# The experts' gate and up weights, eight neighbouring rows to a partition, and modulated rows stored in the matching order

## The chip, the cores and the metric

The kernel runs on one core of one Trainium2 chip: TensorE (PE in the rows, its weight loads PEld), VectorE (DVE), ScalarE (ACT), GpSimd (POOL), SyncE (SP, which here only issues DMAs), and 16 DMA engines between the device memory and the core's on-chip memory of 128 partitions. The metric is the device time of one execution in microseconds. Before the change it is 4040.15 us, the median of three runs (4038.35 to 4043.37).

## The reference

Three layers work on 1024 tokens of 1024 features, all in float32. Each is a token mixer (neighbourhood attention in the first, grouped-query attention in the second, a mix of three kinds in the third), then a mixture of experts. What matters here is the part between the mixer and the experts, and the experts:

```
y = mixer(h)                                             # ends in @ w_o
x = layer_norm(alpha * x + (1 + g1) * y, ln_g, ln_b)
h = x * (1 + sc2) + sh2                                  # the modulated rows
y = hierarchical_moe(h, ...)

# hierarchical_moe: 32 experts in 4 groups; each token goes to its 2 best
xs = rows of h that the router sends to the expert
ys = (silu(xs @ w_gate[e]) * (xs @ w_up[e])) @ w_down[e]
out = sum over a token's two experts of gate * ys
```

`w_gate` and `w_up` of one expert are 1024x512 in the first two layers and 1024x256 in the third; `w_down` is 512x1024 and 256x1024. The products `xs @ w_gate[e]` and `xs @ w_up[e]` sum over the 1024 features, so any order of the features gives the same result as long as xs and the weights have the same one.

## The kernel before

Matrix products keep float32's precision by splitting each operand into a high and a low part: ACT copies the raw tile to the high part (H), DVE subtracts that from the raw tile for the low part (L), and PE adds three products (`mm3`, lines L181 to L183). In the expert stages ACT's copy is L2237 and DVE's subtraction L2246.

**Weights.** `Experts` holds for each layer a list of 1 MB pieces (`seq`): in the two wide layers (FF = 512) four pieces for gate and up and two for down an expert, in the narrow third layer (FF = 256) two pieces that hold gate and up side by side, and one for down. `load` issues the DMAs of the next piece on SP's queue (L2207, one function for all) into a ring of ten raw tiles R, as soon as an older piece has been split, so loads run some pieces ahead of their use. A piece of gate is 512 rows of the matrix: row k*128 + p of them goes to partition p, so a partition takes four separate rows of 512 floats (2 KB each) or, in the third layer, of 256 floats (1 KB each). `step` runs the matrix products of a piece; chunk q of the features, 128 of them, is on PE's rows.

**Tokens.** The modulated rows h2 lie in device memory. For each expert POOL gathers up to 128 of its tokens' rows (L2257, whole rows of 4 KB), and PE transposes them in eight chunks of 128 features (`turned`), the first chunk being features 0 to 127. If an expert has more than 128 tokens, `extra` runs an extra expert pass (`expert`) behind the stage; with these inputs there is one, in the third layer.

**The mixer's end.** `mixer_out` works through eight tiles of 128 tokens: output projection, layer norm, router. Its inner functions are generators that are advanced between the steps of the projection; the order on each engine is the order in which that code is written, and engines wait for each other by semaphores. Per tile: DVE adds the residual (L475, L478), the layer norm writes z, `modulated` writes h (L510: z times the row A on DVE; L512: plus the row B, on POOL, for the last two tiles on DVE) and stores it to h2 (L513); `last` makes the layer's x in z (L516, L518) and stores it (L519, `x<-z` in the rows). There are two z buffers, so L475 of a tile waits for the store of the tile two before. In the last tile of a routing group (t = 2, 5, 7) DVE runs the routing between these. The rows A and B, the same 1024 numbers in each partition, are made at the start of `mixer_out` by three DVE operations (L418 to L420). The router has weights and columns of its own and reads z, not h2. `ol` (L432) is the low part of the mixer's output, for which PE's first products wait.

Of the kernel before, what the change touches and what calls it, by code (L numbers as in the profile page):

```python
# [10 lines left out]
F32 = mybir.dt.float32  # L11
F32R = mybir.dt.float32r
# [4 lines left out]
ALU = mybir.AluOpType  # L17
# [5 lines left out]
P = 128  # L23
T = 1024
D = 1024
NT = T // P
NK = D // P
# [107 lines left out]
class K:  # L135
# [246 lines left out]
    def mixer_out(self, lay, x, ot, x1, h2, hi, pool, first, moe, done):  # L382
# [3 lines left out]
        nc, ps = self.nc, self.ps  # L386
        W, parts, live = {}, {}, []
# [23 lines left out]
        with self.tc.issue_after(ins.ins):  # L411
            G1, A, B = [self.row(q, lay.mod[j * D:(j + 1) * D], f"mod{j}") for q, j in ((first, 2), (pool, 4), (pool, 3))]
            g, b = self.row(pool, lay.ln1_g, "lng"), self.row(pool, lay.ln1_b, "lnb")
            rt = self.router_load(pool, lay, moe.hold)
        nc.vector.tensor_scalar_add(G1, G1, 1.0)

        t1 = pool.tile([P, D], F32, name="z", bufs=2)
        nc.vector.scalar_tensor_tensor(t1, A, 1.0, b, op0=ALU.add, op1=ALU.mult)  # L418
        nc.vector.tensor_add(B, B, t1)
        nc.vector.scalar_tensor_tensor(A, A, 1.0, g, op0=ALU.add, op1=ALU.mult)  # L420
        slots = ps.tile([P, 96], F32, name="R", bufs=1)
        finish, logits = [], []

# [12 lines left out]
        a, c = cols[:, 2], cols[:, 3]  # L436
# [17 lines left out]
        def rest(t, X, Y):  # L454
            s = slice(t * P, (t + 1) * P)
            end = t == NT - 1
            z = pool.tile([P, D], F32, name="z", bufs=2)
            st = pool.tile([P, 20], F32, name="lnst", bufs=4)
            hT = pool.tile([P, NK, P], F32, name="h2T", bufs=1)
            tp, lp = [None, None], []  # L460

            def logit(ks):
                if 0 in ks:
                    lp[:] = [ps.tile([P, 36], F32, name="O", bufs=1)]
                for k in ks:
                    nc.tensor.matmul(lp[0], hT[:, k, :], rw[:, 0, k], start=(k == 0), stop=(k == NK - 1))

            def turned(n):
                tp[n] = ps.tile([P, 4, P], F32, name="tp", bufs=2)
                for k in range(4 * n, 4 * n + 4):  # L470
                    nc.tensor.transpose(tp[n][:, k % 4, :], z[:, k * P:(k + 1) * P], self.ident)

            for n in range(2):
                f = slice(n * 512, (n + 1) * 512)
                nc.vector.tensor_mul(z[:, f], Y[n], G1[:, f])  # L475
                if n == 0:
                    yield
                nc.vector.scalar_tensor_tensor(z[:, f], X[:, f], lay.alpha, z[:, f], op0=ALU.mult, op1=ALU.add)  # L478
                yield
                if n and not end:  # L480
                    yield
                turned(n)
                nc.vector.bn_stats(st[:, 6 * n:6 * n + 6], z[:, f])
                if n == 0:
                    yield
                    nc.scalar.activation(hT[:, 0:4], tp[0], AF.Copy)
                    yield
                    if end:
                        logit(range(4))
            norm = self.normal(z, z, st)  # L490
            next(norm)
            yield
            nc.scalar.activation(hT[:, 4:8], tp[1], AF.Copy)
            next(norm)
            yield
            logit(range(4, 8) if end else range(8))
            next(norm)
            tb = pool.tile([P, 36], F32, name="rtb", bufs=2)
            nc.vector.scalar_tensor_tensor(tb, sums[:, 0], st[:, 17:18], sums[:, 1], op0=ALU.mult, op1=ALU.add)
            if t in starts:  # L500
                logits[:] = [pool.tile([P, 3, 36], F32, name="rL", bufs=2)]
            L = logits[0][:, t - groups[t][0]]
            yield
            run(norm)
            h = pool.tile([P, D], F32, name="h", bufs=1)

            late = t > NT - 3

            def modulated():
                nc.vector.tensor_mul(h, z, A)  # L510
                yield
                (nc.vector if late else nc.gpsimd).tensor_add(h, h, B)  # L512
                (nc.sync if end else nc.gpsimd).dma_start(h2[s], h)  # L513

            def last():
                nc.vector.tensor_mul(z, z, g)  # L516
                yield
                (nc.vector if late else nc.gpsimd).tensor_add(z, z, b)  # L518
                (nc.sync if late else nc.gpsimd).dma_start(x1[s], z)  # L519

            nc.vector.scalar_tensor_tensor(L, lp[0], st[:, 15:16], tb, op0=ALU.mult, op1=ALU.add)
            if t == groups[t][-1]:
                live.append(self.route(groups[t], logits[0], rt, self.tables[lay.l], pool, slots, modulated() if end else iter(())))
            yield
            if not end:
                run(modulated())
            yield
            if late:
                finish.append(last())
            else:  # L530
                run(last())
# [7 lines left out]
        with self.tc.manual_schedule(engines=MANUAL):  # L539
            for t in range(NT):  # L540
# [10 lines left out]
                for i in range(8):  # L551
                    n, j = i // 4, order[i % 4]
                    wh, wl = W[j]
# [541 lines left out]
    def apart(self, key, ins):  # L1095

        for o in self.groups.setdefault(key, []):
            self.tc.declare_no_dep(ins.ins, o.ins, reason="places of their own")
        self.groups[key].append(ins)
# [60 lines left out]
    def expert(self, x, gate, w_gate, w_up, w_down, g2, FF, raw, hi, wk):  # L1160
# [3 lines left out]
        if FF == 512:  # L1164
            for w in (w_gate, w_up):
                for j in range(2):
                    r = next(raw).tile([P, 4, 512], F32, name="R")
                    nc.sync.dma_start(r, w[j * 512:(j + 1) * 512].rearrange("(k p) f -> p k f", p=P))
                    gu.append(r)
        else:  # L1170
            for j in range(2):
                r = next(raw).tile([P, 4, 2, 256], F32, name="R")
                for a, w in enumerate((w_gate, w_up)):
                    nc.sync.dma_start(r[:, :, a], w[j * 512:(j + 1) * 512].rearrange("(k p) f -> p k f", p=P))
                gu.append(r.rearrange("p k a f -> p k (a f)"))
        for j in range(NF // 2):
            r = next(raw).tile([P, 2, D], F32, name="R")
            nc.sync.dma_start(r, w_down[j * 256:(j + 1) * 256].rearrange("(k p) f -> p k f", p=P))
# [8 lines left out]
            self.evac_split(tp, xh[:, 4 * g:4 * g + 4], xl[:, 4 * g:4 * g + 4])  # L1187
        acc = [ps.tile([P, 512], F32, name="pj", bufs=2) for _ in range(len(gu) // 2)]
        for j, r in enumerate(gu):
            wh, wl = self.split(r, *[hi.tile([P, 4, 512], F32R, name=n) for n in "HL"])  # L1190
            o = acc[j // 2]
            for c in range(4):
                k = 4 * (j % 2) + c
                self.mm3(o, xh[:, k], xl[:, k], wh[:, c], wl[:, c], k == 0, k == NK - 1)
        g, u = (acc[0], acc[1]) if FF == 512 else (acc[0][:, :256], acc[0][:, 256:])
        a = wk.tile([P, FF], F32, name="a", bufs=2)
        nc.scalar.activation(a, g, AF.Silu)
# [969 lines left out]
        es.close()  # L2167


class Experts:  # L2170


# [24 lines left out]
    def load(self, queue=None):  # L2197

        i = self.loaded
        place = RING[i % len(RING)]  # L2200
        if i == self.n or place == len(self.raw):
            return
        self.loaded += 1
        raw = self.raw[place]
        kind, e, j = self.seq[i]
        def start(out, in_):
            self.last = (queue or self.nc.sync).dma_start(out, in_)  # L2207

        gate, up, down = self.w
        if kind == "d":  # L2210
            r = raw.tile([P, 2, D], F32, name="R")
            start(r, down[e, j * 256:(j + 1) * 256].rearrange("(k p) f -> p k f", p=P))
        elif self.FF == 512:
            r = raw.tile([P, 4, 512], F32, name="R")
            start(r, (gate, up)[j // 2][e, j % 2 * 512:j % 2 * 512 + 512].rearrange("(k p) f -> p k f", p=P))
        else:
            r = raw.tile([P, 4, 2, 256], F32, name="R")
            for a in range(2):
                start(r[:, :, a], (gate, up)[a][e, j * 512:(j + 1) * 512].rearrange("(k p) f -> p k f", p=P))
            r = r.rearrange("p k a f -> p k (a f)")  # L2220
        self.R[i] = r

    def more(self, pool, px):
# [131 lines left out]
    def step(self, i):  # L2355
        kind, e, j = self.seq[i]
        k = self.k
        (self.wide if self.FF == 512 else self.narrow)(kind, e, j)
        if self.made < i + 4:
            self.make()  # L2360
        wh, wl = self.W.pop(i)
        if kind == "g":
            xh, xl = self.x[e]
            for c in range(4):
                q = 4 * (j % 2) + c
                k.mm3(self.acc[e][j // 2], xh[:, q], xl[:, q], wh[:, c], wl[:, c], q == 0, q == NK - 1)
        else:
            th, tl = self.th[e]
            for c in range(2):
                q = 2 * j + c  # L2370
                for n in range(2):
                    s = slice(n * 512, (n + 1) * 512)
                    k.mm3(self.out[e][n], th[:, q], tl[:, q], wh[:, c, s], wl[:, c, s], q == 0, q == self.NF - 1)
# [210 lines left out]
```

## Time and profile before

| | |
|---|---|
| median of 3 runs | 4040.15 us (4038.35 to 4043.37) |
| profiled execution | 4045.79 us, its span 4044.0 |
| PE busy | 3465.9 us (86%) |
| DVE busy | 3333.8 us (82%) |
| ACT busy | 2284.6 us (56%) |
| POOL busy | 1474.3 us (36%) |
| DMA | 880.07 MB, mean 218 GB/s; 551312 of 554644 packets under 8 KB, 280623 under 2 KB |
| mean granted TensorE clock | 0.925 of full speed |

The span runs from the first to the last instruction. Busy time is summed over an engine's instructions; the stages have different limits, so a share of the whole span does not tell what a stage waits for. In rows of the trace a name left of an arrow is what is written, the names to its right are what is read; a line L510 is a line of the kernel, sometimes of a helper. A number in brackets at the end of a row is how long the engine had been idle, and what ended that.

### The profile page before, as it was taken

Reading aid. Unit: us, or ns where it says so; the run is one execution under the profiler, and the core shown is the slowest. Engines: PE = TensorE matmul, PEld = TensorE weight load, DVE = VectorE, ACT = ScalarE, POOL = GpSimd, SP = SyncE. Lnnn points to the kernel's source line nnn. Section 1 sums busy time; section 2 is a strip of 40 time slices with the busy share of each in tenths; the row PEclk is TensorE's granted clock in tenths of the full one; section 3 lists DMA queues with packets and bytes.
Section 4 is the critical chain, followed back from the end, with each engine's and each line's share of the span. In section 5 each row is a group of like instructions: output and inputs, shape, how many; then the busy total and the mean of one; then the engine's idle time right before and its main releaser. Section 6 shows DMA issues by size and latency. Waiting matters only on the chain. (4 is left out here: it accounts for less than half of the span.)

```text
span 4044.0 us, 50699 instructions
## 1 busy us (share of the span) xinstructions
PE 3465.9 (86%) x17618; PEld 2823.9 (70%) x17618; DVE 3333.8 (82%) x4774; ACT 2284.6 (56%) x3295; POOL 1474.3 (36%) x1138
## 2 busy tenths in 40 slices
PE   5999877799999697999877999993989888869991
PEld 4777756688887576877666888872778666657771
DVE  6599967899998897999777999989445578679996
ACT  3377632577776456888425777764422366237762
POOL 2255413232222335867432322326122142233443
PEclk8999989899999798999998999996979999979996
DMA  8879673899998537434538999995100013559994
GB/s 265 237 142 165 153 184 108 303 379 373 373 376 314 201 123 242 139 115 128 173 107 298 377 369 372 377 335 181 47 14 1 27 50 110 176 163 342 335 350 178
DMA packets 554644, 880.07 MB, mean 218 GB/s; under 512 B 117167, under 2 KB 280623, under 8 KB 551312
## 3 DMA queue, kind: packets, MB, share of 16 engines
q1 hardware_dynamic: 477440, 747.48, 55.5%
q0 software_dynamic: 76944, 129.31, 10.7%
q8 instruction: 141, 2.31, 0.2%
q14 instruction: 119, 0.97, 0.1%
HBM read 791.89 MB, written 126.82 MB: 227 GB/s over the span
## 5 line engine op out<-in xcount | busy, mean ns | idle before, releaser
L2246 DVE TENSOR_TENSOR L<-R,H 128x2048 fp32r<-128x2048 f32 x480 | 1092.7, 2282 | 45.8 <-ACT H L2237 45.3
L2237 ACT ACTIVATE H<-R 128x2048 fp32r<-128x2048 f32 x480 | 918.7, 1916 | 198.5 <-PE R L183 80.6
L2300 POOL DMA_INDIRECT y<-O,slots x96 | 254.9, 2655 | 569.9 <-DVE O L2299 549.6
L2257 POOL DMA_INDIRECT X<-h,slots x87 | 182.0, 2092 | 465.6 <-PE tp L2269 438.8
L181 PE MATMUL pj<-H,xh 128*128 128x512 f32 x776 | 318.6, 411 | 7.9 <-ACT xh L195 5.4
L183 PE MATMUL pj<-H,xl 128*128 128x512 f32 x776 | 308.3, 397 | 19.3 <-DVE xl L196 19.3
L182 PE MATMUL pj<-L,xh 128*128 128x512 f32 x776 | 306.5, 395 | 1.8 <-DVE L L188 1.8
L195 ACT ACTIVATE ph<-tp 128x512 fp32r<-128x512 f32 (+1 forms) x352 | 199.5, 567 | 115.9 <-PE tp L1268 102.6
L359 POOL TENSOR_TENSOR macc<-macc,mw 128x512 f32<-128x512 f32 x182 | 237.1, 1303 | 71.0 <-ACT mw L355 61.6
L196 DVE TENSOR_TENSOR pl<-tp,ph 128x512 fp32r<-128x512 f32 (+1 forms) x352 | 224.7, 645 | 25.3 <-ACT ph L195 23.7
L1252 DVE TENSOR_REDUCE st<-S 128x1 f32<-128x1024 f32 (+2 forms) x192 | 204.1, 1063 | 21.5 <-PE S L1558 18.6
L181 PE MATMUL S<-H,xh 128*128 128x512 f32 x512 | 211.9, 414 | 0.0
L195 ACT ACTIVATE xh<-tp 128x512 fp32r<-128x512 f32 x194 | 115.4, 597 | 166.4 <-PE tp L2269 103.5
L183 PE MATMUL S<-H,xl 128*128 128x512 f32 x512 | 201.7, 394 | 0.0
L182 PE MATMUL S<-L,xh 128*128 128x512 f32 x512 | 199.6, 390 | 0.0
L183 PEld LDWEIGHTS pj<-H,xl 128*128 128x128 f32 x776 | 147.8, 190 | 53.9 <-DVE xl L196 20.7
L181 PEld LDWEIGHTS pj<-H,xh 128*128 128x128 f32 x776 | 148.3, 191 | 35.9 <-ACT xh L195 6.2
L1268 PE MATMUL tp<-ident,E 128*128 128x128 f32 x1111 | 171.7, 273 | 0.5 <-DVE pl L196 0.5
L1279 PE MATMUL O<-ph,V 128*128 128x512 f32 (+1 forms) x352 | 163.2, 464 | 10.4 <-DVE U L1286 10.4
L182 PEld LDWEIGHTS pj<-L,xh 128*128 128x128 f32 x776 | 148.6, 191 | 30.3 <-DVE L L188 2.1
L1268 PEld LDWEIGHTS tp<-ident,E 128*128 128x128 f32 x1111 | 139.2, 141 | 37.0 <-DVE pl L196 1.7
L1262 ACT ACTIVATE E<-S,st 128x1024 f32<-128x1024 f32 (+6 forms) x149 | 157.1, 1054 | 12.0 <-DVE st L1252 10.8
(592 smaller groups left out, 9877.7 us busy)
## 6 DMA issues: line engine op xcount, KB each, us to landing
R<-moe_w_down SPq DMA_DIRECT2D x161, 1024.0 KB
R<-moe_w_up SPq DMA_DIRECT2D x127, 1024.0 KB
R<-moe_w_gate SPq DMA_DIRECT2D x126, 1024.0 KB
mw<-ada_w SPq DMA_DIRECT2D x160, 256.0 KB
R<-moe_w_gate SPq DMA_DIRECT2D x66, 512.0 KB
R<-moe_w_up SPq DMA_DIRECT2D x66, 512.0 KB
Y<-y SPq DMA_DIRECT2D x24, 1024.0 KB
mw<-w_mod SPq DMA_DIRECT2D x96, 256.0 KB
```

The source lines that it names most:

```text
L181: mm(out, ah, bh, start=first, stop=False)
L182: mm(out, ah, bl, start=False, stop=False)
L183: mm(out, al, bh, start=False, stop=last)
L195: nc.scalar.activation(hi, src, AF.Copy)
L196: nc.vector.tensor_sub(lo, src, hi.bitcast(F32))
L359: nc.gpsimd.tensor_add(acc, acc, W)
L1252: nc.vector.tensor_reduce(blk.st[:, a, 0:1], S[:, :n], axis=AX.X, op=ALU.max, negate=True)
L1268: nc.tensor.transpose(tp[:, a, :], blk.E[a][:, c * P:(c + 1) * P], self.ident)
L2237: self.nc.scalar.activation(hi, r, AF.Copy)
L2246: self.nc.vector.tensor_sub(lo, r, hi.bitcast(F32))
L2257: return self.nc.gpsimd.indirect_dma_start(out=self.X[e % 3], out_offset=None, in_=self.h2d, in_offset=IOA(ap=i, axis=0), bounds_check=T - ...
L2300: ins = nc.gpsimd.indirect_dma_start(out=self.y, out_offset=IOA(ap=self.slots.bitcast(I32)[:, 1, e:e + 1], axis=0), in_=O, in_offset=None, ...
```

## The change

Row 8p + k of gate or up, instead of row k*128 + p, goes to partition p: a partition holds eight neighbouring rows, which come in two pieces of four. The four rows are one stretch in device memory, 8 KB in the wide layers and 4 KB in the third, where gate and up now lie one behind the other in the raw tile (2, 4, 256) instead of side by side (4, 2, 256), and PE's moving operand is two runs of 256 columns. Chunk k of the features is then 8p + k for p = 0 to 127. For the tokens' rows to match, `modulated` writes h in eight pieces of 128, piece k from every eighth number of z; A and B are brought into that order once a layer by two copies, and the sums that A and B come from are made in the tile z first. Down weights are as before. The same is done in the extra pass.

```diff
         t1 = pool.tile([P, D], F32, name="z", bufs=2)
+        apart = lambda v: v.rearrange("t (p k) -> t k p", k=NK)
+        pieces = lambda v: v.rearrange("t (k p) -> t k p", k=NK)
         nc.vector.scalar_tensor_tensor(t1, A, 1.0, b, op0=ALU.add, op1=ALU.mult)
-        nc.vector.tensor_add(B, B, t1)
-        nc.vector.scalar_tensor_tensor(A, A, 1.0, g, op0=ALU.add, op1=ALU.mult)
+        nc.vector.tensor_add(t1, t1, B)
+        nc.vector.tensor_copy(pieces(B), apart(t1))
+        t1 = pool.tile([P, D], F32, name="z", bufs=2)
+        nc.vector.scalar_tensor_tensor(t1, A, 1.0, g, op0=ALU.add, op1=ALU.mult)
+        nc.vector.tensor_copy(pieces(A), apart(t1))
...
             def modulated():
-                nc.vector.tensor_mul(h, z, A)
+                nc.vector.tensor_mul(pieces(h), apart(z), pieces(A))
...
+def rows_of(w, j):
+    return w.rearrange("(p k) f -> p k f", k=NK)[:, 4 * j:4 * j + 4]
...
         elif self.FF == 512:
             r = raw.tile([P, 4, 512], F32, name="R")
-            start(r, (gate, up)[j // 2][e, j % 2 * 512:j % 2 * 512 + 512].rearrange("(k p) f -> p k f", p=P))
+            start(r, rows_of((gate, up)[j // 2][e], j % 2))
         else:
-            r = raw.tile([P, 4, 2, 256], F32, name="R")
+            r = raw.tile([P, 2, 4, 256], F32, name="R")
             for a in range(2):
-                start(r[:, :, a], (gate, up)[a][e, j * 512:(j + 1) * 512].rearrange("(k p) f -> p k f", p=P))
-            r = r.rearrange("p k a f -> p k (a f)")
+                start(r[:, a], rows_of((gate, up)[a][e], j))
...
-                k.mm3(self.acc[e][j // 2], xh[:, q], xl[:, q], wh[:, c], wl[:, c], q == 0, q == NK - 1)
+                w = [v[:, c] if self.FF == 512 else v[:, :, c] for v in (wh, wl)]
+                k.mm3(self.acc[e][j // 2], xh[:, q], xl[:, q], *w, q == 0, q == NK - 1)
```

The order of instructions changes on DVE at the start of each `mixer_out` alone. The second layer's start on DVE, before; `mod_18608` is the row A, `mod_18610` the row B, `rab` and `rcols` belong to the router:

```order
L188 TENSOR_TENSOR L<-R,H 128x2048 x4
L418 SCALAR_TENSOR_TENSOR z<-mod_18608,lnb 128x1024
L438 SCALAR_TENSOR_TENSOR rab<-rcols 128x8
L432 TENSOR_TENSOR ol<-o,oh 128x512
L419 TENSOR_TENSOR mod_18610<-mod_18610,z 128x1024
L420 SCALAR_TENSOR_TENSOR mod_18608<-mod_18608,lng 128x1024
L439 TENSOR_TENSOR rcols<-rcols,rab 128x8
```

The same place with the change, where A is `mod_18611` and B `mod_18613`, and `ol` has the line L438:

```order
L188 TENSOR_TENSOR L<-R,H 128x2048 x4
L421 SCALAR_TENSOR_TENSOR z<-mod_18611,lnb 128x1024
L425 SCALAR_TENSOR_TENSOR z<-mod_18611,lng 128x1024
L422 TENSOR_TENSOR z<-z,mod_18613 128x1024
L426 COPY mod_18611<-z 128x1024
L423 COPY mod_18613<-z 128x1024
L444 SCALAR_TENSOR_TENSOR rab<-rcols 128x8
L438 TENSOR_TENSOR ol<-o,oh 128x512
```

Two copies are new, and all five operations on the rows stand ahead of `ol`, of which one did before. In the first layer the operations on the rows and the router's stood ahead of `ol` already. On DVE there, before:

```order
L418 SCALAR_TENSOR_TENSOR z<-mod_5367,lnb 128x1024
L841 TENSOR_TENSOR U<-O,U 64x256
L419 TENSOR_TENSOR mod_5369<-mod_5369,z 128x1024
L843 TENSOR_TENSOR OT<-O,U 64x16x16
L420 SCALAR_TENSOR_TENSOR mod_5367<-mod_5367,lng 128x1024
L438 SCALAR_TENSOR_TENSOR rab<-rcols 128x8
L841 TENSOR_TENSOR U<-O,U 64x256
```

and with the change:

```order
L421 SCALAR_TENSOR_TENSOR z<-mod_5367,lnb 128x1024
L847 TENSOR_TENSOR U<-O,U 64x256
L422 TENSOR_TENSOR z<-z,mod_5369 128x1024
L849 TENSOR_TENSOR OT<-O,U 64x16x16
L423 COPY mod_5369<-z 128x1024
L425 SCALAR_TENSOR_TENSOR z<-mod_5367,lng 128x1024
L847 TENSOR_TENSOR U<-O,U 64x256
L426 COPY mod_5367<-z 128x1024
```

Here the two copies come in between the last attention steps (U, OT), and the router's rows move behind them. The third layer's start changes as the second's, but there nothing of the four split parts (L188) stands ahead. On SP no instruction moves: the six loads of gate and up at the third layer's start still stand ahead of the load of `o` (L398), with a shape of 128x1024 instead of 128x4x256. PE and ACT have the same order as before.

## Rows read from the trace of the kernel before

**Rows 1.** Windows, all engines: us; busy us (xinstructions) each; PE clock, DMA share, GB/s.
```profile
842.70:1144.96 302.26, 302.26 (x1429) 249.63 (x1429) 292.09 (x205) 228.77 (x171) 85.81 (x34) 1.00 1.02 373
...
3684.70:3860.77 176.07, 173.39 (x834) 138.51 (x833) 176.07 (x163) 130.51 (x126) 76.35 (x37) 1.00 1.00 340
3860.77:3914.69 53.92, 50.23 (x235) 38.67 (x233) 49.55 (x46) 36.77 (x37) 24.05 (x10) 1.00 1.01 343
...
3446.00:3456.00 10.00, 2.94 (x22) 2.58 (x20) 0.16 (x1) 0.00 (x0) 0.00 (x0) 0.82 1.07 341
...
10.00:40.00 30.00, 9.19 (x48) 8.86 (x48) 22.27 (x30) 13.03 (x34) 8.56 (x6) 0.93 1.05 387
...
3400.00:3404.00 4.00, 4.00 (x26) 3.36 (x25) 3.77 (x8) 2.92 (x7) 0.00 (x0) 1.00 1.02 417
```

**Rows 2.** Waits of ACT and DVE, 3860 to 3915: us, times, longest.
```profile
ACT H L2237 <- DMA R<-moe_w_up: 8.9, 8, 1.7
ACT H L2237 <- DMA R<-moe_w_down: 6.0, 5, 1.5
...
DVE L L2246 <- ACT H L2237: 4.4, 7, 1.0
```

**Rows 3.** Timelines of SP, ACT, DVE, 3438 to 3460: start, us.
```profile
3443.03 0.43 SPq L2207 DMA_DIRECT2D R<-moe_w_gate  x1
...
3448.56 1.37 SPq L398 DMA_DIRECT2D o<-ot  x1
...
3456.79 1.06 ACT L428 ACTIVATE oh<-o 128x1024 fp32r<-128x1024 f32 x1 [22.28 <-DMA o<-ot]
...
3457.88 1.22 DVE L432 TENSOR_TENSOR ol<-o,oh 128x1024 fp32r<-128x1024 f32 x1 [11.72 <-ACT oh L428]
```

**Rows 4.** Waits of ACT, 3950 to 3956; of POOL and DVE, 695 to 735.
```profile
ACT H L187 <- DMA R<-moe_w_down: 1.1, 1, 1.1
...
POOL X L2257 <- DMA h<-h: 13.6, 1, 13.6
...
DVE xl L196 <- DMA x<-z: 10.6, 1, 10.6
```

**Rows 5.** Lines by source: durations in ns, shortest/median/longest.
```profile
L843 DVE TENSOR_TENSOR OT<-O,U x64: 590/642/699, 209.7 to 547.4; 64x256 f32<-64x256 f32 x64
...
L841 DVE TENSOR_TENSOR U<-O,U x64: 407/410/417, 209.3 to 546.8; 64x256 f32<-64x256 f32 x64
...
L744 DVE TENSOR_TENSOR Q<-pj,Q x32: 1102/1175/1274, 183.0 to 493.4; 64x512 fp32r<-64x512 f32 x32
...
L746 DVE SCALAR_TENSOR_TENSOR KL<-pj,KH x32: 677/689/696, 170.8 to 472.6; 64x512 fp32r<-64x512 f32 x32
...
L510 DVE TENSOR_TENSOR h<-z,mod x24: 1214/1218/1224, 581.0 to 3589.1; 128x1024 f32<-128x1024 f32 x24
...
L2552 DVE TENSOR_SCALAR g<-g x3: 684/684/684, 735.7 to 3624.7; 128x1024 f32<-128x1024 f32 x3
```

**Rows 6.** Timelines of DVE and POOL, 590 to 612; last, idle of L475.
```profile
593.86 0.69 DVE L475 TENSOR_TENSOR z<-pj,mod 128x512 f32<-128x512 f32 x1 [1.91 <-DMA x<-z]
...
596.37 1.22 DVE L510 TENSOR_TENSOR h<-z,mod 128x1024 f32<-128x1024 f32 x1
...
609.10 0.69 DVE L475 TENSOR_TENSOR z<-pj,mod 128x512 f32<-128x512 f32 x1 [1.85 <-DMA x<-z]
...
597.67 2.39 POOL L512 TENSOR_TENSOR h<-h,mod 128x1024 f32<-128x1024 f32 x1 [8.42 <-DVE h L510]
...
DMA x<-z: 43.5, 11
```

**Rows 7.** Timelines of DVE and PE at the first and second mixer's end.
```profile
546.79 0.42 DVE L841 TENSOR_TENSOR U<-O,U 64x256 f32<-64x256 f32 x1 [0.84 <-ACT U L832]
...
558.44 0.79 PE L183 MATMUL pj<-H,ol 128*128 128x512 f32 x1 [2.30 <-DVE ol L432]
...
1972.19 0.79 PE L183 MATMUL pj<-H,ol 128*128 128x512 f32 x1 [3.36 <-DVE ol L432]
```

More of the change, by code (lines that the diff above doesn't have):

```diff
@@ L1167, in expert @@
                     r = next(raw).tile([P, 4, 512], F32, name="R")
-                    nc.sync.dma_start(r, w[j * 512:(j + 1) * 512].rearrange("(k p) f -> p k f", p=P))
+                    nc.sync.dma_start(r, rows_of(w, j))
                     gu.append(r)
@@ L1171, in expert @@
             for j in range(2):
-                r = next(raw).tile([P, 4, 2, 256], F32, name="R")
+                r = next(raw).tile([P, 2, 4, 256], F32, name="R")
                 for a, w in enumerate((w_gate, w_up)):
-                    nc.sync.dma_start(r[:, :, a], w[j * 512:(j + 1) * 512].rearrange("(k p) f -> p k f", p=P))
-                gu.append(r.rearrange("p k a f -> p k (a f)"))
+                    nc.sync.dma_start(r[:, a], rows_of(w, j))
+                gu.append(r)
         for j in range(NF // 2):
@@ L1189, in expert @@
         for j, r in enumerate(gu):
-            wh, wl = self.split(r, *[hi.tile([P, 4, 512], F32R, name=n) for n in "HL"])
+            parts = self.split(r, *[hi.tile(list(r.shape), F32R, name=n) for n in "HL"])
             o = acc[j // 2]
@@ L1193, in expert @@
                 k = 4 * (j % 2) + c
-                self.mm3(o, xh[:, k], xl[:, k], wh[:, c], wl[:, c], k == 0, k == NK - 1)
+                w = [v[:, c] if FF == 512 else v[:, :, c] for v in parts]
+                self.mm3(o, xh[:, k], xl[:, k], *w, k == 0, k == NK - 1)
         g, u = (acc[0], acc[1]) if FF == 512 else (acc[0][:, :256], acc[0][:, 256:])
```

## The prediction, made before the changed kernel had run

> **What bounds the kernel now.** I read the page first, then the windows of the stages in which the touched weights stream, then the waits of ScalarE (ACT) and VectorE (DVE) there, and last the timelines of the three mixer stages, where the modulated rows are made. PE is busy 86% of the span and DVE 82%, so an average says little; each stage has its own limit.
>
> In the windows [rows 1] the wide expert stages (512 hidden columns) belong to PE: from 842.70 to 1144.96 it is busy in all of 302.26 us, DVE in 292.09, and the DMA engines are full (share 1.02, 373 GB/s). A weight that lands sooner there finds nobody waiting. The narrow stage (256 columns) belongs to DVE: 176.07 of 176.07. Only at its end does it starve: in the 53.92 us from 3860.77 DVE works 49.55, so 4.4 are idle, and the waits of that stretch say why [rows 2]: DVE waits 4.4 us for the high halves (H) of ACT, which itself waits 8.9 and 6.0 for raw weights. 343 GB/s is not enough there. That is where faster loads pay in full.
>
> What the loads can gain is in the same windows [rows 1]: 1 KB pieces (third layer's gate and up, with little else moving) go at 341 GB/s, 2 KB pieces at 387, 4 KB pieces at 417; the share is over 1 in all three, so these are what full queues deliver. The step from 1 to 4 KB is worth a fifth, from 2 to 8 KB a few per cent.
>
> **What the change removes.** Narrow tail: gate and up are 2 MB of an expert's 3; at 417 instead of 341 GB/s these take 5.0 instead of 6.2 us, 1.1 an expert. An expert here is 46 matmuls (24 for gate and up, 12 for down, 10 transposes), so the tail's 235 are five experts: 5.6 us, more than the 4.4 of DVE idle. So −4.4, and DVE is the limit again. Third layer's start: SP issues six gate and up loads (3 MB) from 3443.03 on, ahead of the `o` load at 3448.56, and ACT waits 22.28 us for `o` until 3456.79, DVE and PE behind it [rows 3]. 3 MB take 9.2 us at 341 GB/s and 7.5 at 417: −1.7. The extra expert behind the last stage waits 1.1 for its down weights, queued behind its gate and up loads [rows 4]: −1.1. At the start of each expert stage the gather waits 13.6 for the stored rows and DVE 10.6 for stored x [rows 4], with weight loads in the same engines. If a whole 10 us of each were load traffic, 7% (387 to 417) in two layers and twice that in the third would be 2.8; not all of it is, so I take half, −1.4, with 0 and −12 as bounds (the rival below). In the wide stages nothing. Together −8.6.
>
> A rule speaks against any gain: the Trainium skill, "DMA: Bandwidth & Descriptors", Specifications, puts the smallest transfer at line rate at 512 B, so 1 KB pieces would have lost nothing and the sum would lose its 8.6 on the credit side. The rows of 341, 387 and 417 GB/s disagree with that; what it would do here is rival B.
>
> **What it adds: the strided read.** h is now written in order of the new layout (in eight pieces of 128) from z read at every eighth float, 32 bytes apart: 24 instructions, 8 tiles in 3 layers, 1.218 us each before [rows 5]. No row shows such a read from SBUF by itself. Nearest rows, with some operand at a 32-byte step: DVE 64x256 goes from 410 to 642 ns (0.91 ns an element; one operand is in PSUM), and DVE 64x512 from 689 to 1175 (0.95; read and written so). Two forms, nearly one price: 0.93 ns on average x 1024 = 0.95 us, so 2.17 instead of 1.22. Bounds: nothing added if only the PSUM side or the write pays, and a doubling (+1.2). Below nothing is excluded: the same elements are read and no operation leaves. I take +0.95, the value that both rows give.
>
> For this one the Trainium skill has a rule, "SBUF — State Buffer", Specifications (TRN2): an SBUF line is 16 bytes, and an access that finds only one hit in each line pays. Every read here lands in another line, so by it the read is charged, as in my sum; no row here shows the read alone.
>
> Do the 24 stand on the path? The timeline of the mixer stage [rows 6]: L510 at 596.37, then POOL's addition L512 (which waited 8.42 for it), POOL's store, L518, the x<-z store, and DVE's L475 of two tiles on waits 1.85 for that store at 609.10, since there are two z buffers. The whole loop hangs on L510: idle of L475 for the store is 43.5 us in 11 of its 48 instructions, so POOL and the store set the pace, and a later L512 moves each of them. In the other tiles L510 stands in DVE's own row between the layer norm and the routing, and the last tile of a layer goes L510, addition, store, gather, PE: on the path as well [rows 4]. What of this is not on the path I can't read from a row; the forecast charges all. 24 x 0.95 = +22.8.
>
> **The copies.** A and B must be in the new order too: in each layer two copies with a strided read and nothing else. A one-input operation of 128x1024 takes 0.684 [rows 5] and a two-input one 1.22; a strided copy lies between 0.69 (free) and 1.22 + 0.95 = 2.17. I take 2.15, the price of the strided product. First layer: they stand in DVE's queue ahead of the four low parts and `ol`, for which PE waits 2.30 at 558.44; 0.84 us of DVE idle there takes some up [rows 7]: 2 x 2.15 − 0.84 = +3.5. Second layer: only L418 and `rab` stood ahead of `ol` and PE waited 3.36 for it; in the new order two more 1.2 us operations and both copies come ahead of it: 2.4 + 4.3 = +6.7 [rows 7]. Third layer: DVE sits idle before `ol` behind ACT's 22.28 [rows 3], and everything is absorbed: 0. Were that cover gone, 6.7 again.
>
> Other edits: the matmul's moving operand in the third layer is two runs of 256 instead of one of 512; DVE binds there and PE has slack (173.39 of 176.07), so 0. ACT's and DVE's conversions keep a contiguous 128x2048. The gather takes whole 4 KB rows as before.
>
> **Sum.** 22.8 + 3.5 + 6.7 − 8.6 = +24.4. The profiled execution took 4045.79 us (span 4044.0), 5.6 over the median of 4040.15; on its own time 4070.2, on the median **4064.5**.
>
> **Rivals.**
> (A) The strided read from SBUF is free: the charge of rows 5 belonged to PSUM or to writes. For: both rows have such an operand; against: two different forms, nearly one price. Then only the copies cost, at 0.69 to 1.22: first layer 0.5 to 1.6, second 3.8 to 4.8, on average 5.3, and 8.6 come back: 4040.15 − 3.3 = 4037, not slower.
> (B) Strides as forecast, but larger pieces give nothing, because the 341 GB/s was the mix of the moment: +33.0, 4073. Against: the three speeds are ordered by piece.
> (C) On the other side: the waits behind stores at the stage starts [rows 4] are load traffic that drains much faster, 4 us in each of three stages, 12 instead of 1.4. It decides when the read is below some 0.4 us: with it free, 4037 − 10.6 = 4026, faster; with it charged, 4054. Against: bytes and queues stay as they are.
>
> **How the numbers follow.** Forecast 0.66, A 0.18, B 0.08, C with a free read 0.04, the rest 0.04. A measurement here can tell 0.2%, 8.1 us, from no change: below 4032.1 is faster, above 4048.2 slower. Slower: forecast, B and a little of the rest, 0.75; A for most of its weight falls within, 0.14; C and A's lower tail are faster, 0.11. The forecast's own range is 4050 (gains twice mine, stride a little less) to 4078 (stride at its upper bound, no gain). For 8 in 10 it must reach to A, down to 4034.
>
> **What would show it.** L510 at 2.1 to 2.2 us instead of 1.22, 24 times, and the tile loop of 15.2 us (593.86 to 609.10) some 0.95 longer; six copies of about 2 us ahead of `ol` and PE's waits of 2.30 and 3.36 grown to about 6 and 10; the loads' speed at the third layer's start near 417 GB/s; DVE without idle in the narrow tail. If L510 stays at 1.22, A or C is right. If L510 is slow and the loop no longer, DVE had slack that I didn't see.

## The result: slower by 0.6%, as forecast

The changed kernel takes 4062.07 us (median of 6 runs, 4056.36 to 4069.11) beside 4039.25 for the kernel before on the same chip: ratio 1.0062, 95% interval 1.0044 to 1.0079. The forecast was 4064.5. Its profiled execution took 4069.11 us with a span of 4067.2, 23.2 longer than that of before. A row here has the line numbers of its own kernel: L510 is now L516, L512 L518, L475 L481, L2299 L2310.

The product and the copies, by source line (ns, shortest/median/longest), after:

```profile
L516 DVE TENSOR_TENSOR h<-z,mod x24: 1994/2152/2185, 580.6 to 3614.7; 128x1024 f32<-128x1024 f32 x24
...
L423 DVE COPY mod<-z x3: 1074/1081/1090, 542.8 to 3463.1; 128x1024 f32<-128x1024 f32 x3
...
L426 DVE COPY mod<-z x3: 1074/1076/1077, 545.3 to 3462.1; 128x1024 f32<-128x1024 f32 x3
```

The product went from 1.218 to 2.152 us [rows 5], +0.93 against +0.95 forecast. The copies take 1.08, half of what I gave them. The tile loop of [rows 6], after (timelines of DVE and POOL):

```profile
594.41 0.69 DVE L481 TENSOR_TENSOR z<-pj,mod 128x512 f32<-128x512 f32 x1 [1.93 <-DMA x<-z]
...
596.91 2.17 DVE L516 TENSOR_TENSOR h<-z,mod 128x1024 f32<-128x1024 f32 x1
...
610.69 0.69 DVE L481 TENSOR_TENSOR z<-pj,mod 128x512 f32<-128x512 f32 x1 [1.84 <-DMA x<-z]
...
599.18 2.39 POOL L518 TENSOR_TENSOR h<-h,mod 128x1024 f32<-128x1024 f32 x1 [9.40 <-DVE h L516]
```

POOL waits 9.40 for the product instead of 8.42, DVE still 1.84 for the store at the end, and the loop is 16.28 us instead of 15.24: the later product moves everything behind it. The windows that answer to [rows 1], after:

```profile
838.00:1140.20 302.20, 302.20 (x1429) 249.58 (x1428) 292.03 (x205) 228.82 (x171) 83.50 (x34) 1.00 1.00 386
...
3711.60:3887.70 176.10, 173.54 (x834) 138.55 (x834) 176.10 (x163) 132.18 (x128) 76.19 (x37) 1.00 0.99 371
3887.70:3941.60 53.90, 52.88 (x255) 41.85 (x254) 53.90 (x51) 39.63 (x40) 22.60 (x11) 1.00 0.94 354
```

The loads did get faster: 386 instead of 373 GB/s and 371 instead of 340 in stages that take the same time, since PE and DVE bind there. In the narrow tail DVE is busy in all of 53.90, where it had 49.55 of 53.92. ACT's waits for raw weights (47.7 us for up alone over the whole execution before) are gone from the list of waits.

For the stages I took, in each trace, the time between starts of the same DVE instructions (us). Tiles: from the residual of the second tile to that of the eighth, three layers; 18 of the 24 products stand in these stretches. Start 1, start 2: from the first operation on the rows A and B to the first residual of that layer. Wide tails: from the 21st to the last expert's output, two layers; narrow tail: the same of the third. Mixer 3: from there in the second layer to the first operation on A in the third, which no kernel here changes. The rows below the second are the experiments; e_steps, whose step differs by layer, is left out.

| kernel | tiles | start 1 | start 2 | wide tails | narrow tail | mixer 3 |
|---|---|---|---|---|---|---|
| before | 326.6 | 21.1 | 6.6 | 361.0 | 97.2 | 716.8 |
| after | 350.4 | 22.5 | 10.9 | 357.0 | 94.4 | 722.5 |
| e_again | 349.2 | 21.0 | 10.4 | 357.0 | 93.1 | 701.1 |
| e_ctrl | 323.7 | 19.8 | 7.5 | 362.3 | 96.6 | 697.7 |
| e_rows | 347.7 | 22.5 | 10.9 | 361.0 | 96.6 | 700.9 |
| e_loads | 325.7 | 21.2 | 5.4 | 357.1 | 92.1 | 714.1 |
| e_write | 342.5 | 21.4 | 6.6 | 357.0 | 93.7 | 714.3 |
| e_two | 323.2 | 21.7 | 10.1 | 357.0 | 93.3 | 715.3 |
| e_pe | 327.9 | 21.2 | 6.5 | 357.6 | 93.6 | 698.0 |
| e_pe2 | 324.0 | 21.2 | 6.6 | 357.6 | 95.5 | 712.7 |
| e_pe_two | 325.0 | 21.1 | 6.7 | 358.3 | 95.3 | 715.0 |

### The profile page after: what moved, and what is told of

Its sections match the earlier page's. It is cut to its first block, busy times and chain, and to the rows that moved or that the text cites. A ratio compares the mean times of both kernels' runs of the same rounds, so it can differ in the third digit from the quotient of the medians.

```text
span 4067.2 us, 50708 instructions
## 1 busy us (share of the span) xinstructions
PE 3484.6 (86%) x17618; PEld 2841.0 (70%) x17618; DVE 3363.9 (83%) x4780; ACT 2286.1 (56%) x3295; POOL 1477.4 (36%) x1138
## 5 line engine op out<-in xcount | busy, mean ns | idle before, releaser
L1286 PE MATMUL O<-ph,V 128*128 128x512 f32 (+1 forms) x352 | 163.3, 464 | 10.4 <-DVE U L1293 10.4
L518 POOL TENSOR_TENSOR h<-h,mod 128x1024 f32<-128x1024 f32 x18 | 43.1, 2393 | 343.5 <-DVE h L516 299.3
```

## The experiments

Theory: the step in DVE's read costs 0.93 us in 24 places on the path, the copies a few us more, and the loads give some 8 back at the ends of the expert stages. Rivals: the loads give nothing, or far more; not the read but the new order in memory costs.

(Diffs show the main lines; dots stand for lines left out. They are against the changed kernel, those of e_rows and e_ctrl against the kernel before.)

**e_loads**, the loads without the new order of h; A and B are made as before too:

```diff
-                nc.vector.tensor_mul(pieces(h), apart(z), pieces(A))
+                nc.vector.tensor_mul(h, z, A)
```

> The new weight loads alone: h, A and B stay in the old order, so the experts multiply features that do not belong together. My theory: the larger pieces are worth about 8.6 us as forecast (11 by the two traces), in the tail of the narrow stage (-4.4 to -5), at the third layer's start (-1.7) and where the expert stages start and end, so 4028 to 4031 against 4039 before. Rival: the gains that the traces show at the stage starts are only lateness of the rows that was absorbed there, and the loads alone give 5 or less: 4034 to 4039.

Measured: 0.9916 (0.9898 to 0.9934), 4001.43 us, 34 below before by the ratio (31 by the medians): far more than either theory said. That number can't be taken as it is: see e_ctrl.

**e_rows**, the new order of h with the old loads (and the old tile in the third layer):

```diff
-        nc.vector.tensor_add(B, B, t1)
-        nc.vector.scalar_tensor_tensor(A, A, 1.0, g, op0=ALU.add, op1=ALU.mult)
+        nc.vector.tensor_add(t1, t1, B)
+        nc.vector.tensor_copy(pieces(B), apart(t1))
...
-                nc.vector.tensor_mul(h, z, A)
+                nc.vector.tensor_mul(pieces(h), apart(z), pieces(A))
```

> The modulated rows and A, B in the new order, with the old weight loads, so features do not belong together. My theory: 24 strided products at 2.15 instead of 1.22 us all on the path, +22, and the second layer's copies +4.5, so 4039 + 27 = 4066. Rival: part of the lateness is taken up by the waits at the stage starts (4 us in the first layer alone), so 4058 to 4061.

Measured: 0.9992 (0.9974 to 1.0011), 4029.39 us. Taken alone it would say that the step costs nothing, although the table has the tiles 21 us longer.

**e_ctrl**, what other data do to the time:

```diff
-            start(r, (gate, up)[j // 2][e, j % 2 * 512:j % 2 * 512 + 512].rearrange("(k p) f -> p k f", p=P))
+            start(r, (gate, up)[j // 2][e, (1 - j % 2) * 512:(1 - j % 2) * 512 + 512].rearrange("(k p) f -> p k f", p=P))
...
```

> The kernel before with the two halves of the gate and up rows swapped, so that features do not belong together, as in e_loads and e_rows. The traces of these two lack the extra expert pass (46 matmuls) behind the third layer's experts: other data, other routing. Theory: that alone is 25 us (from the last expert to the end 66.8 us in them, 92.1 in the kernel before), and this kernel lacks it too: 0.9937 of before; the loads alone are then 5 to 9 us and the rows alone +20 to +24. Rival: the extra pass is worth less, this kernel runs at 0.998 or more, and the loads alone are worth 20 us or more.

Measured: 0.9944 (0.9923 to 0.9965). The busy line of the page of the profile, of e_loads and of e_ctrl:

```profile
PE 3442.0 (86%) x17572; PEld 2804.7 (70%) x17572; DVE 3323.6 (83%) x4765; ACT 2276.9 (57%) x3288; POOL 1471.2 (37%) x1136
```

```profile
PE 3441.5 (86%) x17572; PEld 2799.7 (70%) x17572; DVE 3323.5 (83%) x4765; ACT 2278.4 (57%) x3288; POOL 1471.4 (37%) x1136
```

Both have 17572 matmuls, 46 less than before: the extra expert pass is missing. With other values in the second and third layer the routing differs, and I take it that no expert has more than 128 tokens there. From the last expert's output to the end it is 66.8 us in e_loads, e_rows and e_ctrl and 92.1 in before: the pass is worth 25 us. Against this control the loads alone are 0.9916/0.9944, −0.28% or −11 us, and the rows alone 0.9992/0.9944, +0.48% or +19 us, each give or take 0.28% or 11 us. So the rival's 0.998 for this kernel is refuted, and the step does cost; but the loads' 11 us are at the edge of what this can tell from nothing, and the rows' 19 fit the 27 of e_rows' theory and the 19 to 22 of its rival alike. An experiment that spoils the data of a kernel whose work depends on them needs a control that spoils them too.

**e_steps**, the price of the step:

```diff
+        K = (2, 4, 8)[lay.l]
-        apart = lambda v: v.rearrange("t (p k) -> t k p", k=NK)
+        apart = lambda v: v.rearrange("t (p k) -> t k p", k=K)
...
-                nc.vector.tensor_mul(pieces(h), apart(z), pieces(A))
+                nc.vector.tensor_mul(pieces(h), apart(z), (apart if K == NK else pieces)(A))
```

> Prices of the step alone, features do not belong together: as the change, but z is read at every second float (8 bytes) in the first layer, every fourth (16 bytes) in the second, and in the third at every eighth in both z and A. If the price is that of a 16-byte line of which each access finds one number, the product takes 1.22 us at 8 bytes, 2.15 at 16 bytes, and more than 2.15 with two such operands; the copies 0.69, 1.08, 1.08. Rival: any step costs the same, 2.15 us in all three layers.

Measured (timeline of DVE; a copy and the first product of each layer; the one run's time is not used):

```profile
543.00 0.67 DVE L427 COPY mod<-z 128x1024 f32<-128x1024 f32 x1
...
578.01 1.22 DVE L517 TENSOR_TENSOR h<-z,mod 128x1024 f32<-128x1024 f32 x1
...
1965.19 1.06 DVE L427 COPY mod<-z 128x1024 f32<-128x1024 f32 x1
...
2007.96 2.00 DVE L517 TENSOR_TENSOR h<-z,mod 128x1024 f32<-128x1024 f32 x1
...
3429.02 1.11 DVE L427 COPY mod<-z 128x1024 f32<-128x1024 f32 x1
...
3456.11 2.26 DVE L517 TENSOR_TENSOR h<-z,mod 128x1024 f32<-128x1024 f32 x1
```

A step of 8 bytes is free (1.22 and 0.67), and 16 bytes cost nearly what 32 do (2.00). A second operand with a step adds next to nothing: the eight products of the third layer took 2.00 to 2.26, 2.20 in the middle, beside 2.15 with one. So the price begins above 8 bytes and is there at 16. This agrees with the Trainium skill's rule of two hits in a 16-byte line ("SBUF — State Buffer", Specifications (TRN2)), for which the prediction had no row.

**e_write**, the step on the write:

```diff
+        whole = lambda v: v.rearrange("t (p k) -> t p k", k=NK)
...
-                nc.vector.tensor_mul(pieces(h), apart(z), pieces(A))
+                nc.vector.tensor_mul(h.rearrange("t (k p) -> t p k", k=NK), whole(z), whole(A))
```

> As the change, but the product reads z and A in their own order and writes h in the new one: the step (512 bytes) is on the write. A stays as it was, only B is copied. If the read's step alone makes the price, the product is back at 1.22 us, the tile loops are as before, and the loads' gain less about 2 us of the copy is left: 0.997 to 0.999 of before. If a write with a step costs as much, it takes 2.15 us and the kernel is at 1.004 to 1.006, little below the change.

Measured: 1.0054 (1.0034 to 1.0075), the product by source line:

```profile
L515 DVE TENSOR_TENSOR h<-z,mod x24: 1902/2006/2024, 579.8 to 3592.9; 128x1024 f32<-128x1024 f32 x24
```

A write with a step costs nearly as much, 2.01; that the read alone pays is refuted, and the tiles stay 16 us longer than before. Between these two, 32 bytes on the read and 512 on the write, it matters little which side of the product takes the step.

**e_two**, two neighbouring rows to a partition instead of eight (pieces of 4 and 2 KB), z read at 8 bytes:

```diff
-        apart = lambda v: v.rearrange("t (p k) -> t k p", k=NK)
+        apart = lambda v: v.rearrange("t (p k) -> t k p", k=2)
...
-    return w.rearrange("(p k) f -> p k f", k=NK)[:, 4 * j:4 * j + 4]
+    return w[j * 512:(j + 1) * 512].rearrange("(b p k) f -> p b k f", p=P, k=2)
```

> The change with two neighbouring rows to a partition instead of eight: pieces of 4 KB in the wide layers and 2 KB in the third, z read at every second float (8 bytes), features in agreement again. By the prices of e_steps the product is 1.22 us and a copy 0.69, so the tile loops are as before; the second mixer's start costs 2.4 + 1.4 = 3.8, the first 0.5, and the loads give back most of their 8 us (the tails of the wide stages 3 and 1, of the narrow one 3). Theory: 0.998 to 1.000 of before, 20 us below the change. Rival: the stores of h or the copies, not the product, made the change slower: 1.004.

Measured: 0.9993 (0.9979 to 1.0008), with this row:

```profile
L516 DVE TENSOR_TENSOR h<-z,mod x24: 1216/1220/1225, 581.5 to 3574.5; 128x1024 f32<-128x1024 f32 x24
```

The product is back at 1.22, the tiles at 323.2, and the wide tails are as short as with 8 KB; the rival's 1.004 is outside the interval. What the change lost in the tiles was the step in the read. The 4 us at the second layer's start are lost here too (10.1 instead of 6.6).

**e_pe** and, once more, **e_pe2**: h, A and B as before, the new order made by PE's transposes of the gathered rows:

```diff
-            self.nc.tensor.transpose(tp[:, c, :], src[:, (4 * g + c) * P:(4 * g + c + 1) * P], k.ident)
+            q = 4 * g + c
+            s = src[:, q * P:(q + 1) * P] if step == 1 else src.rearrange("t (p k) -> t k p", k=step)[:, q]
+            self.nc.tensor.transpose(tp[:, c, :], s, k.ident)
...
-            self.turned(self.X[e % 3], g, 4, self.x[e])
+            self.turned(self.X[e % 3], g, 4, self.x[e], NK)
```

> New loads as in the change, but h, A and B stay in the old order in memory; the new order of the features is made where PE transposes the gathered rows, by reading every eighth feature as the weights of the transpose. If PE reads a 32-byte step without a price, this costs nothing and keeps the whole gain of the loads: 4028 to 4031, faster than both kernels. If PE pays for the step as VectorE does (a weight load of 0.14 us doubled, 8 a expert, in the wide stages where PE is the limit), 64 x 8 x 0.14 = 72 us: up to 4100.

> e_pe once more: by its trace the product is as before, the weight load of a gathered chunk takes 0.190 instead of 0.140 us with PE's matmul beside it, and the stages around the third layer's mixer are 7 us shorter than before. Theory: 0.998 of before, 7 us faster. Rival: PE's dearer weight load or the mixer stages take it back: 1.000, as in the first five rounds (0.9995).

Measured: 0.9995 (0.9979 to 1.0011), then 0.9982 (0.9966 to 0.9999).

**e_pe_two**: the same with two neighbouring rows.

> e_pe with two neighbouring rows to a partition: PE reads the gathered rows at every second float when it transposes them, VectorE works as before. If PE's weight load has the same price list as VectorE's reads, it is back at 0.140 us (0.190 at 32 bytes); the wide stages lose the 0.5 us that e_pe had more. Theory: 0.998 of before, like e_pe. Rival: pieces of 4 and 2 KB give less of the loads' gain: 1.000.

Measured: 0.9982 (0.9967 to 0.9997). PE's load of a gathered chunk by source line, of before, e_pe2 and e_pe_two:

```profile
L2269 PEld LDWEIGHTS tp<-ident,X x768: 137/140/231, 717.9 to 3922.4; 128*128 128x128 f32 x192
```

```profile
L2279 PEld LDWEIGHTS tp<-ident,X x768: 185/191/232, 708.6 to 3899.0; 128*128 128x128 f32 x192
```

```profile
L2289 PEld LDWEIGHTS tp<-ident,X x768: 194/205/231, 716.6 to 3908.2; 128*128 128x128 f32 x192
```

It was 0.140 without a step. PE pays some 0.05 us a load at 32 bytes and 0.065 at 8, so its prices are not DVE's: the load is not doubled at 32 bytes, and not back at 0.140 at 8. Most of it lies beside the matmuls, since the first 20 experts of a wide stage took only 0.5 us longer in e_pe2 (354.3 instead of 353.8) and 1.4 in e_pe_two, where 160 loads of +0.05 would be 8. Both versions beat the changed kernel. Beside the kernel before, e_pe2 and e_pe_two are some 7 us of 4020 faster, at the edge of their intervals, and e_pe, the same kernel as e_pe2, was level; so a gain over before is not settled.

**e_again**, the changed kernel once more:

> The changed kernel once more, for its time beside the others and for a second trace: in the first one the third layer's attention, which the change does not touch, ran 5.2 us longer than before. Theory: that is scatter of one execution and is not there again, or differs by some us; the time is near 4062. Rival: it belongs to the change, and is there again with the same 5 us.

Measured: 1.0052 (1.0035 to 1.0069). Its third mixer took 701.1 us instead of 722.5: scatter, not the change. The same 900 matmuls of that stage (the 601st to the 1500th) in before, after, e_again and e_pe (windows, columns as in [rows 1]):

```profile
2935.86:3090.52 154.66, 142.97 (x901) 128.00 (x903) 68.78 (x173) 39.80 (x82) 36.80 (x46) 0.78 0.04 10
```

```profile
2949.98:3104.65 154.67, 142.99 (x901) 127.97 (x903) 68.79 (x173) 39.83 (x82) 36.83 (x46) 0.78 0.04 10
```

```profile
2948.60:3087.51 138.91, 126.69 (x902) 112.50 (x904) 68.12 (x173) 39.83 (x82) 36.80 (x46) 0.89 0.04 11
```

```profile
2925.59:3060.10 134.51, 121.02 (x902) 106.67 (x903) 67.92 (x173) 39.83 (x82) 36.80 (x46) 0.94 0.05 11
```

The same work took 154.7 us at a mean granted clock of 0.78 and 134.5 at 0.94, and PE's busy time makes up the difference (143.0 and 121.0). 1.00 is the level of 2.4 GHz; the lower means are a mix of it with 1.2. Over the whole stage it was 722.5 us at 0.87 and 698.0 at 0.90.

## Why the prediction was right, step by step

**The product** (+22.8): right in the price and in its place on the path, but the tiles lost more than the price. 18 of the 24 products stand in the tile stretches of the table; at 0.93 they make 16.8 us, and the stretches grew by 22.6 and 23.8 against before and by 24.0 between e_ctrl and e_rows. DVE's busy time in them grew by those 16.8 (255.8 to 272.6 us); the other 6 to 7 are longer waits, for PE's router products (10.7 us before, 14.6 and 13.5 in the two traces of the change) and for the x<-z store (43.5, then 46.2 and 46.5). The first layer's stretch before and after (windows, then DVE's wait for the router products):

```profile
576.75:684.95 108.20, 91.06 (x465) 74.61 (x463) 85.24 (x183) 25.52 (x60) 41.29 (x30) 0.97 0.30 103
...
DVE rL L521 <- PE O L466: 2.8, 2, 1.7
```

```profile
576.39:692.98 116.59, 95.76 (x465) 79.36 (x463) 90.86 (x183) 25.53 (x60) 41.28 (x30) 0.91 0.28 95
...
DVE rL L527 <- PE O L472: 5.6, 4, 1.7
```

The same matmuls keep PE busy for 95.8 us instead of 91.1, at a mean granted clock of 0.91 instead of 0.97. The granted clock was 0.88 to 0.93 in the stretches of after, e_again, e_rows and e_write, and 0.92 to 0.97 in those of the seven kernels of the table whose product takes 1.22. So where the loop is longer, PE has a lower clock and its products come later; that the one makes the other is argued, not shown. The other six products, in the last two tiles of each layer, show less clearly: from the last tile's residual to the gather it is, over three layers, 79.1 us on average in those seven traces (75.3 to 83.1) and 83.1 in after, e_again and e_rows (81.2 to 85.2), +4 where 5.6 was charged. Rival A (the read is free) is refuted by the row of 2.152.

**The copies** (+10.2): mis-sized by half, and in the first layer the wait was another. The step takes a copy from 0.67 (at 8 bytes) to 1.08, not to 2.15: I gave a one-input copy the price of a two-input product. With 1.08 the same working gives 2 x 1.08 − 0.84 = 1.3 in the first layer and 2.4 + 2.2 = 4.6 in the second. Measured: 1.4 and −0.1 in start 1, 4.3 and 3.8 in start 2. In the first layer PE's wait for `ol` did not grow from 2.30 to about 6 (1.91 after); the four low parts ahead of it come later, and PE waits for those, before and after:

```profile
551.23 0.80 PE L182 MATMUL pj<-L,oh 128*128 128x512 f32 x1 [1.83 <-DVE L L188]
```

```profile
550.60 0.80 PE L182 MATMUL pj<-L,oh 128*128 128x512 f32 x1 [3.08 <-DVE L L188]
```

The second layer's start after, on DVE and PE, where the order that [rows 7] had before is replaced:

```profile
1972.89 1.22 DVE L421 SCALAR_TENSOR_TENSOR z<-mod,lnb 128x1024 f32<-128x1024 f32 x1
1974.03 1.22 DVE L425 SCALAR_TENSOR_TENSOR z<-mod,lng 128x1024 f32<-128x1024 f32 x1
1975.16 1.22 DVE L422 TENSOR_TENSOR z<-z,mod 128x1024 f32<-128x1024 f32 x1
1976.30 1.07 DVE L426 COPY mod<-z 128x1024 f32<-128x1024 f32 x1
1977.28 1.08 DVE L423 COPY mod<-z 128x1024 f32<-128x1024 f32 x1
1978.27 0.17 DVE L444 SCALAR_TENSOR_TENSOR rab<-rcols 128x8 f32<-128x8 f32 x1
1978.35 0.69 DVE L438 TENSOR_TENSOR ol<-o,oh 128x512 fp32r<-128x512 f32 x1
...
1979.09 0.80 PE L183 MATMUL pj<-H,ol 128*128 128x512 f32 x1 [7.05 <-DVE ol L438]
```

PE's wait for `ol` grew from 3.36 to 7.05. In the third layer the same five operations were absorbed, as forecast: from the first of them to the second tile's residual it is 26.3 us, and 27.0 before.

**The loads** (−8.6): right in sum, partly wrong in place. The narrow tail: −4.4 forecast, −1.7 to −5.1 in the eight traces with larger pieces, −2.8 and −4.1 in the two of the change. The wide stages, "nothing": wrong, both ended earlier, together by 4.0. The end of the first (windows, columns as in [rows 1]; each ends with the stage), before, with ACT's longest waits in it, and after:

```profile
1213.00:1308.00 95.00, 92.93 (x429) 76.01 (x428) 85.89 (x62) 64.73 (x48) 19.44 (x8) 0.98 0.90 334
...
ACT H L2237 <- DMA R<-moe_w_up: 14.8, 9, 3.2
```

```profile
1213.00:1310.00 97.00, 96.31 (x450) 79.10 (x449) 89.46 (x63) 66.95 (x49) 20.45 (x9) 1.00 0.78 296
```

PE sat idle 2.1 of 95 us there and 0.7 of 97 after. I had looked at the middle of the stage alone, where PE is never idle; at the end ACT waited for weights, because the lead of the loads was used up, and after the change it no longer does. At the third layer's start ACT's `oh` comes 13.1 us after the first weight load's issue instead of 13.8: −0.65, not −1.7. The load rate in the 10 us ahead of it, which was to come near 417 GB/s, was 346 (before it was 341 [rows 1]):

```profile
3464.00:3474.00 10.00, 5.79 (x26) 5.07 (x26) 2.42 (x8) 0.00 (x0) 0.00 (x0) 0.67 1.03 346
```

So the 417 of a 4 us window was not what these loads reach. The extra pass (−1.1) shows no gain above scatter: from the last expert's output to the end it is 91.2 to 93.0 us in the seven traces with larger pieces and this pass, and 92.1 before. Nor do the stage starts (−1.4): from the last tile's residual to the first expert's output it is, over three layers, 251.1 us in before, 247.2 in e_ctrl, and 239.1 to 248.7 in the five traces with larger pieces and the product at 1.22. By the table the tails give −6.8 and −8.1. Rival B (nothing) is refuted by the tails: 357.0 to 358.3 us in all eight traces with larger pieces and 361.0 to 362.3 in the three without, and 92.1 to 95.5 beside 96.6 to 97.2. C with the read charged, 4054 or +14, lies below the intervals of both measurements, of the second by a hair; and in e_two, where the table gives −7.9 for the tails and +4.1 for the starts, 12 us more from the loads would make it some 16 us faster than before, outside its interval, which ends at 8.5.

**The sum.** Tiles, starts and tails of the table come to +22.7 in the first trace and +18.2 in the second, and the last tiles add some 4. The time measured is +25 and +21 by the ratios (+22.8 and +25.3 by the medians; the intervals begin at +17.8 and +14). So +24.4 came out well in part by luck: the copies were some 5 us too dear, and 6 us of waits in the tiles were not in the sum. Of the 23.2 between the two profiled spans 5.7 are the third mixer's scatter.

## What to carry to other kernels

Before a layout is changed to make DMA pieces larger, ask who binds while they land: here that was PE or DVE in nearly the whole of each stage, and faster loads paid only where a lead ran out, at the ends. Then ask which engine makes the new order, how often, and whether that instruction stands on a loop: 0.93 us, 24 times, and the waits that the longer loop brought, outweighed all that the larger pieces gave. The smallest step that gives the DMA enough, two rows and not eight, cost the product nothing; yet with the copies to pay it came out level with the kernel before (0.9993).

## What the runs showed of the hardware

A DVE product of 128x1024 in float32 takes 1.22 us with one input at a step of 8 bytes, as without a step, 2.00 at 16, 2.15 at 32, 2.20 with both inputs at 32 (2.00 to 2.26), and 2.01 with a step of 512 bytes on its output; a copy takes 0.67, 1.06 and 1.08 at 8, 16 and 32. In PE's weight load of 128x128 both steps tried cost: 0.190 us at 32 bytes and 0.205 at 8, beside 0.140. With full DMA queues (share 0.99 to 1.02) the same stages moved 386 GB/s with 8 KB pieces instead of 373 with 2 KB, and 371 with 4 KB instead of 340 with 1 KB. In the third mixer the same 900 matmuls took 154.7 us at a mean granted clock of 0.78 in one execution and 134.5 at 0.94 in another. In the two kernels with two traces each, that stage differed by 21 and 15 us between executions and the spans by 20 and 9: most of the scatter is there.
